# Latent sublayers of a two-layer diffusion trunk: from a raw, then normalised result to an operand normalised in steps behind the first tile pairs

## The chip, the cores and the metric

The kernel runs on one core of a Trainium2 chip. The metric is the device time of one execution in microseconds (us), lower is better. Three runs of the kernel before gave 1200.62, 1200.91 and 1203.27 us; their median is 1200.91 us. One further execution was recorded by the hardware profiler; all rows quoted below come from it.

## What is computed

The reference is a transformer-like trunk with two layers over 256 latent tokens and 256 context tokens of width 1024, all in float32. Each sublayer normalises the stream, scales and shifts it by columns that depend on a conditioning vector, and adds a gated result back:

```
def ffn_sublayer(h, m, g, w13, w2, base):
    hn = modulate(rms_norm(h, g), m[:, :, base], m[:, :, base + 1])
    return h + 0.5 * m[:, :, base + 2] * swiglu(hn, w13, w2)

for i in range(2):
    x = ffn_sublayer(x, ..., 0)          # i = 0: the context too
    x = x + gate * mixer_i(modulate(rms_norm(x)))
    x = ffn_sublayer(x, ..., 6)
return rms_norm(x, final_g)
```

The mixer of layer 0 is windowed attention beside pooling, that of layer 1 a gated three-tap convolution, `W_out(B * conv3(C * x_in))`. The hidden width of a SwiGLU is 2816, or 22 tiles of 128. After layer 0's mixer only the latent tokens are needed, so the last four sublayers (SwiGLU 2 of layer 0, SwiGLU 1 of layer 1, the convolution, SwiGLU 2 of layer 1) work on 256 columns. These four are "latent sublayers"; the change touches only them.

## The kernel before, in words

**Layout.** Everything is transposed: channels lie on the 128 partitions, tokens are the columns of a matmul's moving operand. The stream `x` is `xl_all`, eight blocks (index d or k) of 128 channels by 256 tokens.

**Two-part arithmetic.** The kernel gets float32 accuracy from a faster matmul type (float32r) by splitting each number in two parts, high and low, and adding three products: high·high, high·low and low·high. Weights are split on the chip: `Stream.get` (L80 to L95) hands out weight chunks of 128 x 1024 numbers (eight blocks k of 128 x 128). For each chunk ScalarE casts the raw chunk to `whi` (L100) and VectorE subtracts to get `wlo` (L101). There are four pairs of `whi`/`wlo` buffers, and three raw double chunks in flight from memory on SyncE's queue. So the cast of a chunk can begin when the chunk four places before it has left TensorE, and what it has then is three chunks' time.

**A product of parts, two ways.** `mm3` (L248 to L252) issues three matmuls per block k: `whi` with the operand's high part, `whi` with its low part, `wlo` with the high part. `mm2` (L254 to L261) has the operand's two parts side by side in one tile: one matmul of 512 columns (`whi` with both) and one of 256 (`wlo` with the high part); the two halves of the 512-column result have to be added by whoever reads it. In the last block the 512-column matmul comes last (L261). Before the change `mm2` serves the second half of each SwiGLU (`pz`, L258/L259) and the mixers' output projections (`pwo`).

**Normalising afterwards.** Normalising needs the sum over all channels, known only when the previous sublayer has ended. The first projection of a sublayer does not wait for it: `Act.feed` puts x·gain, not normalised, into the operand tiles `ah` (high) and `al` (low), as soon as a block of the stream is ready, and two further columns 256 and 257 hold the shift. The projections therefore run over 258 columns. The result is normalised when it leaves PSUM: `scaled` (L544 to L550) multiplies by `rs2`, a row of 1/rms per token (1.0 in the two shift columns), and the next instruction adds the shift's product, column 256.

**A SwiGLU (`ffn`).** For f = 0 to 21 ("tile pairs") two chunks, a gate and a value chunk, give `pf`, a PSUM pair (three pairs in turn). `finish` does: `tf` = normalised pair (VectorE, L548), `sl` = Silu (ScalarE, L870), product (VectorE, L871), high part `g` (ScalarE, L872), low part (VectorE, L873). In f = 1 the sums are rooted and spread into `rs2`. Then the second half: for each of eight output blocks d, 22 `mm2` over the pairs `g`, `residual` into `xl_all` (L540) and `feed` of the next sublayer.

**The convolution (`odd_mixer`).** For j = 0 to 7 three chunks: two into `pc` and one into `pb`, then `finish` with `tc`, `zpad`, `y`, `tb`, and an output projection `pwo` of eight blocks of eight `mm2`.

**The modulation columns.** A VectorE dot product (L201, "jk") computes scale, shift and gate columns from weights that stream in by SyncE's queue; a "set" is a load of 1 MB and two such products. 64 sets are spread by credits: `mod_credit(c)` adds c, and a set for the latent tokens costs 2. In `ffn` each pair f from 1 to 21 adds RATE_FFN[0], each chunk of the second half RATE_FFN[1]; in the convolution each j adds RATE_CONV.

**Order.** Inside the latent sublayers the Tile framework's scheduler sets each engine's order from program order, dependencies and priorities (`tc.high_priority`). Each engine takes its instructions in that order.

Of the kernel before, what the change touches and what calls it, by code (L numbers as in the profile page):

```python
# [9 lines left out]
F32 = mybir.dt.float32  # L10
# [7 lines left out]
P = 128  # L18
# [17 lines left out]
NEG = -1e30  # L36
URGENT = 400
RATE_FIRST = (3.3, 1.5)
RATE_FFN = (0.66, 0.7)
RATE_CONV = 0.6  # L40
CH = 8

OPERAND = 4160

C_MODB = 0
C_G = 144
# [71 lines left out]
def hybrid_trunk_kernel(ctx: ExitStack, tc: tile.TileContext, xc, cols_d, modw, wst, poolw_d,  # L118
# [181 lines left out]
    class Act:  # L300
# [39 lines left out]
        def x(self, k, q):  # L340
            return self.hi[:, k, q, :], self.lo[:, k, q, :]

    class Final:
        def __init__(self):
            self.acc = tp.tile([P, 2, T], F32, tag="acc", name="accf", bufs=1)
# [199 lines left out]
    def scaled(pt, rs, n, pool, name):  # L545
        t = pool.tile([P, 544], F32, tag="t", name=f"t{name}", bufs=2)[:, 0:516].rearrange("p (a b) -> p a b", a=2)
        if n:
            nc.vector.tensor_tensor(t[:, 0:n, :], pt[:, 0:n, 0:258], rs, ALU.mult)  # L548
        else:
            nc.vector.tensor_tensor(t[:, 0, :], pt[:, 0:258], rs, ALU.mult)  # L550
        return t

    def lat2(rs):
        return rs[:, 0:1, :].to_broadcast([P, 2, 258])


    def even_mixer(act):
        with tc.tile_pool(name="mix", bufs=2) as ap_:
# [213 lines left out]
            for i in range(4):  # L772
                v = v_turn(i)
                if i + 1 < 4:
                    bias[i + 1] = load_bias(i + 1)
                pr, top, power, weights = scores(i, bias[i])
                if i + 1 < 4:
                    wq = W.get()
                    top(0)
                    top(1)  # L780
                    power(0)
                    power(1)
                    held["q", i + 1] = single(f"pq{i + 1}")
# [12 lines left out]
                    proj_v(i + 1, wv)  # L796
                    po = weigh(i, tn, v)
                    v_finish(i + 1)
                    weigh_finish(i, po)
                    bias_mask(bias[i + 1])  # L800
                    if i == 1:
                        pool_map()
                else:
                    a2 = Act(0, 2, (xl_t,))
# [59 lines left out]
    def ffn(act, l, s, gp, nxt_of, rate1, rate2):  # L864
        g2 = [gp.tile([P, 2, T], F32R, tag=f"g{f}", name=f"g{l}{s}_{f}") for f in range(NF)]

        def finish(f, pt):
            t = scaled(pt, lat2(rs2), 2, gp, f"f{l}{s}{f}")
            sl = gp.tile([P, T], F32, tag="sl", bufs=2, name=f"sl{l}{s}{f}")
            nc.scalar.activation(sl, t[:, 0, 0:256], AF.Silu, bias=t[:, 0, 256:257])  # L870
            nc.vector.scalar_tensor_tensor(sl, t[:, 1, 0:256], t[:, 1, 256:257], sl, ALU.add, ALU.mult)  # L871
            nc.scalar.copy(g2[f][:, 0, :], sl)  # L872
            nc.vector.tensor_tensor(g2[f][:, 1, :], sl, g2[f][:, 0, :].bitcast(F32), ALU.subtract)  # L873

        for f in range(NF):
            pt = pair(f"pf{l}{s}{f}")
            if f == 0:
                ws = W.get(), W.get()
                for ks in (range(KD - 1), range(KD - 1, KD)):
                    for h in range(2):  # L880
                        proj(pt, h, ws[h], act, (0,), ks)
                rr = act.rstd(AF.Silu)
# [24 lines left out]


    def odd_mixer(act, gp, rate):
        y2 = gp.tile([P, KD, 2, T], F32R, name="y2")  # L910
        zs = []
        for b in range(2):
            z = gp.tile([P, T + 32], F32, name=f"zpad{b}")[:, 0 : T + 2]
            nc.gpsimd.memset(z, 0.0)
            zs.append(z)

        def finish(j, pt, pb):
            cw = [cols[:, C_CW + 8 * n + j : C_CW + 8 * n + j + 1] for n in range(3)]
            z = zs[j % 2]
            xi = gp.tile([P, T], F32, tag="sl", bufs=2, name=f"xi{j}")  # L920
            y = gp.tile([P, T], F32, tag="y", bufs=2, name=f"y{j}")
            t = scaled(pt, lat2(rs2), 2, gp, f"c{j}")
            nc.scalar.activation(xi, t[:, 0, 0:256], AF.Identity, bias=t[:, 0, 256:257])
            nc.vector.scalar_tensor_tensor(
                z[:, 1 : T + 1], t[:, 1, 0:256], t[:, 1, 256:257], xi, ALU.add, ALU.mult
            )
# [3 lines left out]
            t = scaled(pb, rs2[:, 0, :], 0, gp, f"b{j}")  # L930
            nc.vector.scalar_tensor_tensor(y, t[:, 0, 0:256], t[:, 0, 256:257], y, ALU.add, ALU.mult)
            nc.scalar.copy(y2[:, j, 0, :], y)
            nc.vector.tensor_tensor(y2[:, j, 1, :], y, y2[:, j, 0, :].bitcast(F32), ALU.subtract)

        for j in range(KD):
            pt, pb = pair(f"pc{j}"), single(f"pb{j}")
            if j == 0:
                ws = W.get(), W.get()
                for ks in (range(KD - 1), range(KD - 1, KD)):
                    for h in range(2):  # L940
                        proj(pt, h, ws[h], act, (0,), ks)
                rr = act.rstd(AF.Silu)
            else:
                for h in range(2):
                    proj(pt, h, W.get(), act, (0,), range(KD))
            w = W.get()
            if j == 0:
                rr.root()
            for k in range(KD):
                mm3(pb[:, 0:258], (w[0][:, k, :], w[1][:, k, :]), act.x(k, 0), k == 0, k == KD - 1)  # L950
            if j == 0:
                rr.spread()
            finish(j, pt, pb)
            mod_credit(rate)
        root_next()
        need_mods(1, 1, 8, 12)
        a2 = Act(1, 2, (xl_t,))
# [6 lines left out]
    act = ffn_first()  # L964
    act = even_mixer(act)
    with tc.tile_pool(name="g1", bufs=1) as gp:
        act = ffn(act, 0, 2, gp, lambda: Act(1, 0, (xl_t,)), *RATE_FFN)
        act = ffn(act, 1, 0, gp, lambda: Act(1, 1, (xl_t,)), *RATE_FFN)
# [134 lines left out]
```

## Time and profile before

| what | value |
|---|---|
| median of three runs | 1200.91 us |
| the profiled execution, its own time | 1201.63 us |
| its span, first to last instruction | 1199.8 us |
| granted TensorE clock, mean over the span | 0.996 |
| weights and other data read | 248.41 MB, 208 GB/s over the span |
| SwiGLU 2 of layer 0, f = 0 to 21 | 517.9 to 652.5 us |
| SwiGLU 1 of layer 1, f = 0 to 21 | 714.5 to 843.0 us |
| convolution, j = 0 to 7 | 905.1 to 975.4 us |
| SwiGLU 2 of layer 1, f = 0 to 21 | 993.2 to 1127.7 us |

How to read the rows: PE is TensorE's matmuls, PEld its weight loads, DVE is VectorE, ACT is ScalarE, SP is SyncE. A row of a timeline gives start, duration, engine, line and operation, and in brackets the idle time before it with what ended it. A matmul's printed duration contains a modelled end and overlaps the next matmul; what a matmul takes of TensorE's time is the distance between starts. A row of grouped instructions ends with count, busy time, mean duration in ns, and the idle time of the engine ahead of them. A row of stages gives for each stretch its length, then each engine's busy time and count, granted clock, share of the DMA engines and GB/s.

### The profile page before, as it was taken

Reading aid. Unit: us, or ns where it says so; the run is one execution under the profiler, and the core shown is the slowest. Engines: PE = TensorE matmul, PEld = TensorE weight load, DVE = VectorE, ACT = ScalarE, POOL = GpSimd, SP = SyncE. Lnnn points to the kernel's source line nnn. Section 1 sums busy time; section 2 is a strip of 40 time slices with the busy share of each in tenths; the row PEclk is TensorE's granted clock in tenths of the full one; section 3 lists DMA queues with packets and bytes.
Section 4 is the critical chain, followed back from the end, with each engine's and each line's share of the span. In section 5 each row is a group of like instructions: output and inputs, shape, how many; then the busy total and the mean of one; then the engine's idle time right before and its main releaser. Section 6 shows DMA issues by size and latency. Waiting matters only on the chain.

```text
span 1199.8 us, 18425 instructions
## 1 busy us (share of the span) xinstructions
PE 1166.3 (97%) x7426; PEld 1041.6 (87%) x7426; DVE 920.2 (77%) x1478; ACT 527.1 (44%) x786; POOL 21.2 (2%) x23
## 2 busy tenths in 40 slices
PE   4999999999999989999999999999999999999997
PEld 2568888888888978789999889999889999999986
DVE  8977686677799577688788988788898888666663
ACT  4352322232344345464445445454545455444542
POOL 2000000000000030000000000000000000000000
PEclk9999999999999999999999999999999999999998
DMA  7764554466676753346776985766884555555541
GB/s 268 256 216 175 176 184 167 156 244 246 265 280 239 204 122 61 106 141 217 260 253 223 335 308 213 262 242 227 306 332 161 207 176 176 178 180 190 189 178 36
DMA packets 45798, 250.65 MB, mean 209 GB/s; under 512 B 12945, under 2 KB 13329, under 8 KB 17553
## 3 DMA queue, kind: packets, MB, share of 16 engines
q1 hardware_dynamic: 45712, 249.48, 59.3%
q8 instruction: 58, 0.95, 0.3%
q14 instruction: 28, 0.22, 0.1%
HBM read 248.41 MB, written 1.05 MB: 208 GB/s over the span
## 4 chain that ended last, share of the span: by engine, by line
PE 93%; DVE 3%; issue 1%; ACT 1%; DMA 0%; SPq 0%; DVEq 0%; ACTq 0%
PE pf L252 11%; PE pf L250 11%; PE pf L251 11%; PE pz L258 10%; PE pa L251 5%; PE pa L252 5%; PE pa L250 5%; PE pz L259 5%; PE p L499 4%; PE py L251 3%; PE py L252 3%; PE py L250 3%; PE pwo L258 1%; PE pc L252 1%; PE pc L250 1%; PE pc L251 1%
## 5 line engine op out<-in xcount | busy, mean ns | idle before, releaser
L100 ACT CAST whi<-raw 128x1024 fp32r<-128x1024 f32 x312 | 327.3, 1050 | 470.9 <-PE pf L251 116.4
L101 DVE TENSOR_TENSOR wlo<-raw,whi 128x1024 fp32r<-128x1024 f32 x312 | 380.1, 1223 | 157.9 <-ACT whi L100 156.7
L252 PE MATMUL pf<-ah,wlo 128*128 128x258 f32 x1056 | 300.9, 285 | 0.0
L250 PE MATMUL pf<-ah,whi 128*128 128x258 f32 x1056 | 300.4, 285 | 0.0
L251 PE MATMUL pf<-al,whi 128*128 128x258 f32 x1056 | 298.2, 282 | 0.0
L201 DVE CUSTOM_DVE_ANT_0 jk<-mr,cvec,cols 128x1024 bf16<-128x1024 f32 x184 | 236.2, 1284 | 2.0 <-DMA mr<-in_modw 0.3
L251 PEld LDWEIGHTS pf<-al,whi 128*128 128x128 f32 x1056 | 202.3, 192 | 0.2
L250 PEld LDWEIGHTS pf<-ah,whi 128*128 128x128 f32 x1056 | 200.7, 190 | 0.0
L252 PEld LDWEIGHTS pf<-ah,wlo 128*128 128x128 f32 x1056 | 200.2, 190 | 0.0
L258 PE MATMUL pz<-g,whi 128*128 128x512 f32 x504 | 178.7, 398 | 0.0
L259 PE MATMUL pz<-g,wlo 128*128 128x256 f32 x528 | 144.3, 281 | 0.0
L258 PEld LDWEIGHTS pz<-g,whi 128*128 128x128 f32 x504 | 94.7, 188 | 22.1
L250 PE MATMUL pa<-xh,whi 128*128 128x512 f32 x288 | 112.0, 389 | 0.0
L252 PE MATMUL pa<-xh,wlo 128*128 128x512 f32 x288 | 112.0, 389 | 0.0
L251 PE MATMUL pa<-xl,whi 128*128 128x512 f32 x288 | 112.0, 389 | 0.0
L259 PEld LDWEIGHTS pz<-g,wlo 128*128 128x128 f32 x528 | 99.7, 189 | 2.2
L250 PE MATMUL py<-gh,whi 128*128 128x512 f32 x176 | 68.5, 389 | 0.0
L251 PE MATMUL py<-gl,whi 128*128 128x512 f32 x176 | 68.5, 389 | 0.0
L252 PE MATMUL py<-gh,wlo 128*128 128x512 f32 x176 | 68.5, 389 | 0.0
L251 PEld LDWEIGHTS pa<-xl,whi 128*128 128x128 f32 x288 | 54.1, 188 | 11.3
L250 PEld LDWEIGHTS pa<-xh,whi 128*128 128x128 f32 x288 | 54.1, 188 | 11.3
L252 PEld LDWEIGHTS pa<-xh,wlo 128*128 128x128 f32 x288 | 54.1, 188 | 11.1
(215 smaller groups left out, 1587.2 us busy)
## 6 DMA issues: line engine op xcount, KB each, us to landing
raw<-in_wst SPq DMA_DIRECT2D x156, 1024.0 KB, 5.1
mr<-in_modw SPq DMA_DIRECT2D x64, 1024.0 KB, 5.1
mr<-in_modw SPq DMA_DIRECT2D x16, 512.0 KB, 5.0
raw<-in_wst SPq DMA_DIRECT2D x8, 512.0 KB, 6.5
bias<-in_rpb SPq DMA_DIRECT2D x32, 64.0 KB, 6.0
xl_all<-in_xc SPq DMA_DIRECT2D x2, 512.0 KB, 7.0
xc_all<-in_xc SPq DMA_DIRECT2D x2, 512.0 KB, 8.4
out<-done SPq DMA_DIRECT2D x3, 256.0 KB, 2.8
```

The source lines that it names most:

```text
L100: nc.scalar.copy(hi, src)
L101: self.last = nc.vector.tensor_tensor(lo, src, hi.bitcast(F32), ALU.subtract).ins
L201: nc.vector.tensor_tensor_reduce(out=junk, in0=raw[:, h, :], in1=cvec[:, q, :], scale=1.0, scalar=cols[:, b : b + 1], op0=ALU.mult, op1=AL ...
L250: nc.tensor.matmul(out, wh, xh, start=first, stop=False)
L251: nc.tensor.matmul(out, wh, xl, start=False, stop=False)
L252: nc.tensor.matmul(out, wl, xh, start=False, stop=last)
L258: nc.tensor.matmul(out, wh, both, start=first, stop=False)
L259: nc.tensor.matmul(out[:, 0:256], wl, x[:, 0, :], start=False, stop=False)
L499: nc.tensor.matmul(pts[j], wf[:, j * P : j * P + P], f32, start=first, stop=last)
```

## The change

`Act` is kept for the parts that also carry context tokens; the latent sublayers use a new class `Lat`.

- `Lat.feed` writes the same x·gain parts, but both into one tile `ah` ("raw").
- `Lat.normalise(d, pool)` makes two blocks (d and d+1) of a normalised operand: multiply the stream by `rs2` (VectorE, 512 elements), scale and shift (two ScalarE activations of 256), high part (ScalarE, 512), low part (VectorE, 512). The parts go side by side into a tile `al`. It is called with d = 0, 2, 4, 6 behind pairs f = 1 to 4 of each SwiGLU and behind j = 0 to 3 of the convolution.
- From pair 6 on (F_RAW), and from j = 4 on (J_RAW), the projection is `wide`: eight `mm2` on that tile. The result needs no normalising and no shift; `joined` adds the two halves: a ScalarE copy out of PSUM and a VectorE addition.
- No credit is given in f = 1 to 5 and j = 0 to 3; the rates become 0.9 per pair (from 0.66) and 1.1 per j (from 0.6).

```
+        def normalise(self, d, pool):
...
+            nc.vector.tensor_tensor(
+                xn, xl_all[:, d : d + 2, :], rs2[:, 0:1, 0:256].to_broadcast([P, 2, T]), ALU.mult
+            )
+            for j in range(2):
+                nc.scalar.activation(
+                    xn[:, j, :], xn[:, j, :], AF.Identity,
+                    bias=mcol[l, s, 0][:, d + j : d + j + 1], scale=gcol[l, s, 0][:, d + j : d + j + 1],
+                )
+            h = self.op[:, d : d + 2, 0, :]
+            nc.scalar.copy(h, xn)
+            nc.vector.tensor_tensor(self.op[:, d : d + 2, 1, :], xn, h.bitcast(F32), ALU.subtract)
+
+    def wide(pt, w, act):
+        for k in range(KD):
+            mm2(pt, (w[0][:, k, :], w[1][:, k, :]), act.op[:, k], k == 0, k == KD - 1)
...
+    def joined(pt, n, pool, name):
+        t = pool.tile([P, 544], F32, tag="t", name=f"t{name}", bufs=2)[:, 0 : n * T].rearrange("p (a b) -> p a b", a=n)
+        nc.scalar.copy(t, pt[:, :, 256:512])
+        nc.vector.tensor_tensor(t, pt[:, :, 0:256], t, ALU.add)
+        return t
...
-RATE_FFN = (0.66, 0.7)
-RATE_CONV = 0.6
+RATE_FFN = (0.9, 0.7)
+RATE_CONV = 1.1
...
             for h in range(2):
                 w = W.get()
                 if f == 1 and h == 0:
                     rr.root()
-                proj(pt, h, w, act, (0,), range(KD))
+                if f < F_RAW:
+                    proj(pt, h, w, act, (0,), range(KD))
+                else:
+                    wide(pt[:, h, :], w, act)
             if f == 1:
                 rr.spread()
                 finish(0, held)
             finish(f, pt)
-            mod_credit(rate1)
+            if 1 <= f <= 4:
+                act.normalise(2 * f - 2, gp)
+            if f >= F_RAW:
+                mod_credit(rate1)
```

**Where instructions stand, TensorE.** The end of the first chunk of pair f = 6 in SwiGLU 2 of layer 0, and the start of its second chunk, in the kernel before (`pf` is the PSUM pair, `ah`/`al` the operand's parts, `whi`/`wlo` the weight's):

```order
L250 MATMUL pf_4618<-ah_3886,whi_4517 128x258
L251 MATMUL pf_4618<-al_3887,whi_4517 128x258
L252 MATMUL pf_4618<-ah_3886,wlo_4518 128x258
L250 MATMUL pf_4618<-ah_3886,whi_4555 128x258
L251 MATMUL pf_4618<-al_3887,whi_4555 128x258
L252 MATMUL pf_4618<-ah_3886,wlo_4556 128x258
```

The same place in the changed kernel, where `al` now holds both parts of the normalised operand:

```order
L260 MATMUL pf_4635<-al_4346,whi_4528 128x512
L261 MATMUL pf_4635<-al_4346,wlo_4529 128x256 x2
L263 MATMUL pf_4635<-al_4346,whi_4528 128x512
L260 MATMUL pf_4635<-al_4346,whi_4572 128x512
L261 MATMUL pf_4635<-al_4346,wlo_4573 128x256
```

Three matmuls of 258 columns per block have become one of 512 and one of 256; nothing else moved in between.

**VectorE at the convolution's fourth group.** The last part of j = 3 in the kernel before (`tc`, `tb` come out of PSUM, `zpad` and `y` are the convolution, `wlo` the weight split):

```order
L548 TENSOR_TENSOR tc_8838<-pc_8748,rs_97 128x516
L101 TENSOR_TENSOR wlo_8809<-raw_8646,whi_8808 128x1024
L924 SCALAR_TENSOR_TENSOR zpad_8419<-tc_8838,xi_8836 128x256
L927 TENSOR_SCALAR y_8837<-zpad_8419,cols 128x256
L550 TENSOR_TENSOR tb_8845<-pb_8749,rs_97 128x258
L929 SCALAR_TENSOR_TENSOR y_8837<-zpad_8419,cols,y_8837 128x256 x2
L101 TENSOR_TENSOR wlo_8855<-raw_8646,whi_8854 128x1024
L931 SCALAR_TENSOR_TENSOR y_8837<-tb_8845,y_8837 128x256
```

The same in the changed kernel, where L390 and L400 are the first and the last instruction of the step that normalises blocks 6 and 7:

```order
L1012 TENSOR_SCALAR y_8415<-zpad_7986,cols 128x256
L613 TENSOR_TENSOR tb_8423<-pb_8327,rs_97 128x258
L1014 SCALAR_TENSOR_TENSOR y_8415<-zpad_7986,cols,y_8415 128x256
L390 TENSOR_TENSOR xn_8428<-xl_all,rs_97 128x512
L1014 SCALAR_TENSOR_TENSOR y_8415<-zpad_7986,cols,y_8415 128x256
L103 TENSOR_TENSOR wlo_8439<-raw_8218,whi_8438 128x1024
L1017 SCALAR_TENSOR_TENSOR y_8415<-tb_8423,y_8415 128x256
L400 TENSOR_TENSOR al_8101<-xn_8428,al_8101 128x2x256
```

The normalising step stands behind `tb`, which reads the group's last PSUM result, and ahead of the group j = 4 that needs it.

**TensorE at the convolution's fifth group.** In the kernel before the two chunks of `pc` in j = 4 follow each other:

```order
L250 MATMUL pc_8850<-ah_7828,whi_8750 128x258
L251 MATMUL pc_8850<-al_7829,whi_8750 128x258
L252 MATMUL pc_8850<-ah_7828,wlo_8751 128x258
L250 MATMUL pc_8850<-ah_7828,whi_8780 128x258
L251 MATMUL pc_8850<-al_7829,whi_8780 128x258
```

In the changed kernel six blocks of the first `pc` chunk are followed by six of the `pb` chunk, and only then by blocks 6 and 7 of `pc`:

```order
L260 MATMUL pb_8435<-al_8101,whi_8386 128x512
L261 MATMUL pb_8435<-al_8101,wlo_8387 128x256
L260 MATMUL pc_8434<-al_8101,whi_8328 128x512
L261 MATMUL pc_8434<-al_8101,wlo_8329 128x256 x2
L263 MATMUL pc_8434<-al_8101,whi_8328 128x512
L260 MATMUL pc_8434<-al_8101,whi_8358 128x512
```

So twelve blocks' matmuls, not six, stand between the group's start and the first use of operand blocks 6 and 7.

More of the change, by code (lines that the diff above doesn't have):

```diff
@@ L341, in x, with __init__, feed, rstd @@
             return self.hi[:, k, q, :], self.lo[:, k, q, :]
+    class Lat:
+        def __init__(self, l, s):
+            need_mods(l, s, 0, 8)
+            self.l, self.s, self.name = l, s, f"{l}{s}"
+            self.raw = xp.tile([P, OPERAND], F32R, tag="ah", name=f"ah{l}{s}")[:, 0 : KD * 516].rearrange(
+                "p (k a t) -> p k a t", k=KD, a=2)
+            self.acc = tp.tile([P, 2, T], F32, tag="acc", name=f"acc{l}{s}", bufs=1)
+            sh = mcol[l, s, 0][:, 0:8].unsqueeze(2).to_broadcast([P, KD, 2])
+            h = self.raw[:, :, 0, 256:258]
+            nc.scalar.copy(h, sh)
+            nc.vector.tensor_tensor(self.raw[:, :, 1, 256:258], sh, h.bitcast(F32), ALU.subtract)
+        def feed(self, d):
+            with tc.high_priority(offset=URGENT):
+                x = xl_t[d]
+                g = gcol[self.l, self.s, 0][:, d : d + 1]
+                h = self.raw[:, d, 0, 0:256]
+                acc = self.acc[:, 0, :]
+                sq = acc if d == 0 else tp.tile([P, T], F32, tag="sq0", name=f"sq{self.name}0{d}", bufs=2)
+                nc.scalar.activation(h, x, AF.Copy, scale=g)
+                nc.vector.scalar_tensor_tensor(
+                    self.raw[:, d, 1, 0:256], x, g, h.bitcast(F32), ALU.mult, ALU.subtract
+                )
+                nc.scalar.activation(sq, x, AF.Square)
+                if d:
+                    nc.vector.tensor_tensor(acc, acc, sq, ALU.add)
+        def rstd(self):
+            return Rstd([self.acc[:, 0, :]], 256, self.name, AF.Silu)
+        def x(self, k, q):
+            return self.raw[:, k, 0, :], self.raw[:, k, 1, :]
+        def normalise(self, d, pool):
+            l, s = self.l, self.s
+            if d == 0:
+                self.op = xp.tile([P, OPERAND], F32R, tag="al", name=f"al{l}{s}")[:, 0 : KD * 512].rearrange(
+                    "p (k a t) -> p k a t", k=KD, a=2)
+            xn = pool.tile([P, 544], F32, tag="t", name=f"xn{l}{s}{d}", bufs=2)[:, 0:512].rearrange(
+                "p (a b) -> p a b", a=2)
+            nc.vector.tensor_tensor(
[5 more added lines that the diff above has]
+                    bias=mcol[l, s, 0][:, d + j : d + j + 1], scale=gcol[l, s, 0][:, d + j : d + j + 1],
+                )
+            h = self.op[:, d : d + 2, 0, :]
+            nc.scalar.copy(h, xn)
+            nc.vector.tensor_tensor(self.op[:, d : d + 2, 1, :], xn, h.bitcast(F32), ALU.subtract)
@@ L888, in ffn @@
                     rr.root()
-                proj(pt, h, w, act, (0,), range(KD))
+                if f < F_RAW:
+                    proj(pt, h, w, act, (0,), range(KD))
+                else:
+                    wide(pt[:, h, :], w, act)
             if f == 1:
@@ L941, in odd_mixer @@
                         proj(pt, h, ws[h], act, (0,), ks)
-                rr = act.rstd(AF.Silu)
+                rr = act.rstd()
+            elif j < J_RAW:
+                for h in range(2):
+                    proj(pt, h, W.get(), act, (0,), range(KD))
             else:
                 for h in range(2):
-                    proj(pt, h, W.get(), act, (0,), range(KD))
+                    wide(pt[:, h, :], W.get(), act)
             w = W.get()
@@ L948, in odd_mixer @@
                 rr.root()
-            for k in range(KD):
-                mm3(pb[:, 0:258], (w[0][:, k, :], w[1][:, k, :]), act.x(k, 0), k == 0, k == KD - 1)
+            if j < J_RAW:
+                for k in range(KD):
+                    mm3(pb[:, 0:258], (w[0][:, k, :], w[1][:, k, :]), act.x(k, 0), k == 0, k == KD - 1)
+            else:
+                wide(pb, w, act)
             if j == 0:
@@ L953, in odd_mixer @@
             finish(j, pt, pb)
-            mod_credit(rate)
+            if j < 4:
+                act.normalise(2 * j, gp)
+            if j >= J_RAW:
+                mod_credit(rate)
         root_next()
         need_mods(1, 1, 8, 12)
-        a2 = Act(1, 2, (xl_t,))
+        a2 = Lat(1, 2)
         proj_out = OutProj(y2, 1, a2, ODD_OUT)
```

43 lines of the change are left out of this document (28 added, 15 removed).

## The prediction

> **What bounds the kernel now.** I read the page first (busy shares and the chain that ended last), then the stages, then TensorE's starts inside stages.
>
> ```profile
> PE 1166.3 (97%) x7426; PEld 1041.6 (87%) x7426; DVE 920.2 (77%) x1478; ACT 527.1 (44%) x786; POOL 21.2 (2%) x23
> PE 93%; DVE 3%; issue 1%; ACT 1%; DMA 0%; SPq 0%; DVEq 0%; ACTq 0%
> ```
>
> TensorE is busy nearly all the time and carries 93% of the chain. Since matmuls overlap, "busy" does not yet say that none waits; for that I look at the latent sublayers stage by stage: pairs f = 2 to 5 of SwiGLU 2 of layer 0, its later pairs, its second half, then the convolution's j = 1 to 3 and j = 4 to 7.
>
> ```profile
> core 0: us, PE busy (x) PEld busy (x) DVE busy (x) ACT busy (x) POOL busy (x), PEclk, DMA share, GB/s
> 536.40:559.60 23.20, 23.20 (x194) 23.20 (x194) 18.59 (x27) 11.87 (x18) 0.00 (x0) 1.00 0.65 228
> 565.50:652.40 86.90, 86.90 (x720) 86.90 (x719) 70.01 (x105) 42.68 (x60) 0.00 (x0) 1.00 0.68 242
> 652.50:714.50 62.00, 62.00 (x354) 53.89 (x353) 57.16 (x93) 31.09 (x41) 0.00 (x0) 1.00 0.88 319
> 914.36:940.52 26.16, 26.16 (x219) 26.16 (x217) 24.32 (x42) 12.24 (x17) 0.00 (x0) 1.00 0.56 189
> 940.52:975.40 34.88, 34.88 (x291) 34.88 (x289) 27.90 (x45) 15.46 (x20) 0.00 (x0) 1.00 0.52 181
> ```
>
> In each, TensorE's busy time equals the stretch and the granted clock is 1.00. VectorE is next, with 80% to 93%. Does anything else set the pace? The waits of the weight stream say no:
>
> ```profile
> ACT whi L100 <- PE pf L251: 116.4, 76, 1.8
> ACT whi L100 <- PE pz L258: 63.0, 42, 1.8
> ```
>
> ScalarE's cast of a weight chunk waits for TensorE to release a buffer, not the other way round. So in these stages time is the number of matmuls times their distance, and that is where the change acts.
>
> **The distance of the two matmul patterns.** Now the starts. First a stretch of the old pattern, three matmuls of 258 columns per block: a group of the convolution, j = 1.
>
> ```profile
> 914.36 0.29 PE L250 MATMUL pc<-ah,whi 128*128 128x258 f32 x1
> ...
> 923.08 0.29 PE L250 MATMUL pc<-ah,whi 128*128 128x258 f32 x1
> ```
>
> Between these starts lie three chunks of eight blocks, 72 matmuls: 8.72 us, so 2.907 us per chunk. The pattern of one 512 and one 256 exists in two places. The last two whole output blocks of the convolution's projection (8 blocks k each):
>
> ```profile
> 987.40 0.40 PE L261 MATMUL pwo<-y,whi 128*128 128x512 f32 x1
> ...
> 993.01 0.40 PE L261 MATMUL pwo<-y,whi 128*128 128x512 f32 x1
> ```
>
> 5.61 us for 16 blocks, or 2.805 us per eight. And the whole second half of SwiGLU 1 of layer 1, 8 x 22 = 176 blocks:
>
> ```profile
> 843.00 0.40 PE L258 MATMUL pz<-g,whi 128*128 128x512 f32 x1
> ...
> 905.06 0.28 PE L250 MATMUL pc<-ah,whi 128*128 128x258 f32 x1
> ```
>
> 62.06 us, or 2.821 us per eight. Weights, chunk layout and the position of the last 512-column matmul in `pwo` are those of the new projections, so I lean to it and take 2.81 us.
>
> **The change, part by part.**
>
> *New projections.* Pairs 6 to 21 are 16 pairs of 2 chunks in three SwiGLUs, 96 chunks; j = 4 to 7 are 4 groups of 3, 12 chunks. 108 chunks x (2.907 - 2.81) = 10.5 us less; by `pz` 9.3, by `pwo` 11.0. All of it lies on the path that sets the end as long as TensorE stays the engine waited for. Where does the gain come from? Not mainly from columns: 774 become 768 per block, 0.8%, while the rows give 3%. One matmul start fewer per block carries the rest. The Trainium skill ("TensorE: Matmul & The Clock Gate", section "Back-to-back issue gap") gives the distance of warm matmuls as N/2.4 + 2.5 ns; an estimate from it is that a block goes from 330 to 325 ns and the 864 blocks gain 4.3 us instead of 10.5. The trace disagrees with it in size: it has 363 ns (2.907 us / 8) and 351 ns.
>
> *The normalising steps.* Durations of the nearest forms, and of what stands in each pair already:
>
> ```profile
> L101 DVE TENSOR_TENSOR wlo<-raw,whi 128x1024 fp32r<-128x1024 f32 x312 | 380.1, 1223 | 157.9 <-ACT whi L100 156.7
> L100 ACT CAST whi<-raw 128x1024 fp32r<-128x1024 f32 x312 | 327.3, 1050 | 470.9 <-PE pf L251 116.4 <-PE pa L251 114.1 <-PE pz L258 63.0
> L201 DVE CUSTOM_DVE_ANT_0 jk<-mr,cvec,cols 128x1024 bf16<-128x1024 f32 x184 | 236.2, 1284 | 2.0 <-DMA mr<-in_modw 0.3
> L548 DVE TENSOR_TENSOR tf<-pf,rs 128x516 f32<-128x516 f32 x66 | 45.8, 694 | 21.5 <-PE pf L252 20.5 <-ACT rs L296 0.9
> L871 DVE SCALAR_TENSOR_TENSOR sl<-tf,sl 128x256 f32<-128x256 f32 x66 | 31.6, 479 | 0.0
> L873 DVE TENSOR_TENSOR g<-sl,g 128x256 fp32r<-128x256 f32 x66 | 27.9, 423 | 21.3 <-ACT g L872 21.3
> L439 DVE TENSOR_TENSOR s<-s,pa 128x512 f32<-128x512 f32 x18 | 12.3, 682 | 0.0
> L441 DVE TENSOR_TENSOR gl<-s,gh 128x512 fp32r<-128x512 f32 x22 | 15.1, 686 | 3.5 <-ACT gh L440 3.4
> L440 ACT CAST gh<-s 128x512 fp32r<-128x512 f32 x22 | 13.7, 622 | 24.9 <-DVE s L439 24.9
> L438 ACT ACTIVATE s<-pa 128x512 f32<-128x512 f32 x18 | 10.6, 589 | 0.0
> L328 ACT ACTIVATE ah<-xl_all,g 128x256 fp32r<-128x256 f32 x40 | 20.3, 509 | 27.9 <-DVE xl_all L529 14.7 <-DVE xl_all L540 13.1
> ```
>
> One step is two VectorE operations of 512 (2 x 0.686 = 1.37 us) and on ScalarE 2 x 0.509 + 0.622 = 1.64 us. Sixteen steps put 22 us on VectorE and 26 us on ScalarE, beside TensorE's matmuls. What hides them is VectorE's spare time, and it has to be enough in that stage: in f = 2 to 5, 18.59 us of 23.20 are used, with one modulation set (2 x 1.284 = 2.6 us) that is moved away; 18.59 - 2.6 + 4 x 1.37 = 21.5 us (all four steps run in this stretch), 93%. In the convolution's j = 1 to 3 it is tight: 24.32 - 2.6 + 3 x 1.37 (the fourth step runs in j = 4) = 25.8 of 26.16 us, 99%. Overlapping starts make the real load a little less, queue waits make it more. VectorE takes its instructions in order, so behind each step's last subtraction (it waits for two activations and a cast on ScalarE) stand the next `wlo` and the parts of `g` or `y`. The reserve against that is the four weight buffers: a cast released at the end of a chunk is needed three chunks, 8.7 us, later.
>
> *The entry into the new operand.* In a SwiGLU the last step stands behind pair 4 and pair 6 begins a whole pair (5.8 us) later: no wait. In the convolution it stands behind `tb`, which waits for the end of j = 3: then about 0.4 us `tb`, 0.5 `y`, 0.7 the multiplication, 1.0 two activations, 0.6 cast, 0.7 subtraction, 3.9 us, and on VectorE meanwhile two more `y` operations and a `wlo`. TensorE first does twelve blocks, 12 x 0.351 = 4.2 us. If VectorE is late, which 99% makes likely, one wait follows. I bound it by 0 and 2.5 us (two late `wlo`) and take 1.0.
>
> *The result of pairs 6 and later.* VectorE: `tf` with 0.694 becomes an addition of 512 out of PSUM (0.68), `sl` a plain product, nearer the 0.423 of L873 than 0.479: about 0.1 us less per pair. ScalarE gets a copy of 512 out of PSUM, 0.59 us, and has room for it: 42.68 of 86.90 us. But it stands in ScalarE's queue ahead of a weight cast, and waits for the pair's end. The way from there is 0.59 + 1.05 (cast) + 0.68 + 1.22 (`wlo`) = 3.5 us, with a modulation set between 6.1, and the chunk is needed after 8.4 us. No wait; the last pair's way to `g` is longer by that 0.59 and is needed only 21 blocks, 7.4 us, after the pair.
>
> *Modulation sets.* Their number stays 64. From pair 6 on 0.9 of credit is 0.45 set per pair. VectorE's own part there: 70.01 us less five sets at 2.6 over 15 pairs is 3.8 us per pair; with 0.45 x 2.6 it is 5.0 of the new 5.62 us, 89%. The second half already runs at 57.16 of 62.00 us, 92%, with TensorE never waiting, so this is bearable. SyncE's queue gets the loads of 1 MB later and closer; the 242 GB/s of the stage rise towards 270, below the 319 of the second half.
>
> *The raw parts in one tile, the two shift columns:* same bytes, same instructions, no cost. The rest of the kernel is unchanged.
>
> **Sum.** -10.5 + 1.0 = -9.5 us. Against the profiled execution (1201.63 us, of which the span is 1199.8) that is 1192.1 us; this execution lay 0.72 us above the median, so I predict 1191.4 us for the median.
>
> **The rivals.** *Lost at the entries (0.10).* VectorE falls behind in the steps and TensorE waits at all four entries, or the weights come late behind them. At 1.0 to 1.5 us each, 4 to 6 us are lost: 1200.9 - 10.5 + 4 to 6 = 1194.4 to 1196.4 us. For it: 99% in the convolution, the new ScalarE round trip in each pair. Against: the pair of reserve in the SwiGLUs and the second half, which runs without a wait at the same load.
>
> *Only columns count (0.05).* If the new projections ran at the old price per column, because their operand tile behaves unlike `pwo`'s, the gain is 108 x 2.907 x 6/774 = 2.4 us, and with the wait of 1.0 us the time is 1199.5 us: no difference. Against it stand both measured stretches. The rule of the Trainium skill cited above ("TensorE: Matmul & The Clock Gate") points this way, with its 4.3 us.
>
> *The weight stream runs dry (0.04), slower.* Place: pairs with a modulation set. VectorE's load there is 3.8 + 2.6 = 6.4 us, and its addition now waits for ScalarE's copy, 0.59: 7.0 us against 5.62, 1.4 more than the pair gives; normally the next pair makes up for it. If the reserve were gone, each of the 15 sets (14 in two SwiGLUs, one in the convolution) would stop TensorE by 1.4 us, 21 us in all: 1200.9 - 10.5 + 21 = 1211.4 us, slower. It decides from the point where the way of 6.1 us exceeds 8.4, that is with 2.3 us of further queueing. Against it: the second half carries 92% without a wait.
>
> **How the numbers follow.** Forecast 0.81, with a range of its own from 1189.2 (by `pwo`, no wait, and 0.7 us for the runs' spread) to 1193.5 (by `pz`, a wait of 2). The range to hold the time 8 in 10 goes from 1189.0 to 1195.5: it leaves out the last two rivals, most of the first, and small tails. A measurement of this kernel can tell about 0.2%, 2.4 us, from no change. Below 1198.5 lie the forecast, the first rival and part of the doubt: faster 0.91, same 0.05, slower 0.04.
>
> **What would show it.** Right: starts of consecutive first matmuls of pairs 6 to 21 lie 5.6 us apart (5.81 before), VectorE near 93% in f = 2 to 5 and 89% in later pairs, casts still waiting for TensorE. A gap of TensorE at j = 4 between 0 and 2.5 us and none at pair 6. Wrong: TensorE's gaps ahead of `al` in pair 6, or ahead of `wlo` in pairs with a set; or 2.88 us per new chunk without any gap. The prediction falls if the time is above 1198.5 us.

## The result and the profile after

The changed kernel takes 1190.74 us (median of four runs, 1190.12 to 1193.23) against 1201.21 us for four runs of the kernel before: ratio 0.9914, 95% interval 0.9895 to 0.9932. It is faster by 10.5 us, or 0.9%; the prediction was 1191.4. (Of all executions reported below one, of the kernel with the padded operand, took 2188 us at a granted clock of 0.86; it is left out of every comparison.) The profiled execution took 1190.12 us with a span of 1188.3, 11.5 us less than before's span. I account for the change against these two spans, where the starts of single instructions can be compared.

The profile page of the changed kernel, busy times and chain:

```profile
PE 1155.3 (97%) x6562; PEld 990.7 (83%) x6562; DVE 930.9 (78%) x1510; ACT 572.8 (48%) x886; POOL 21.2 (2%) x23
PE 93%; DVE 3%; issue 1%; ACT 1%; DMA 0%; SPq 0%; DVEq 0%; ACTq 0%
```

864 matmuls fewer, and TensorE still carries 93% of the chain. The stages that the prediction read, in the same order (pairs 2 to 5, later pairs, second half, j = 1 to 3, j = 4 to 7):

```profile
535.58:558.46 22.88, 22.88 (x194) 22.88 (x193) 20.68 (x30) 18.39 (x30) 0.00 (x0) 1.00 0.59 203
564.10:648.60 84.50, 84.50 (x481) 73.51 (x480) 70.63 (x110) 48.77 (x76) 0.00 (x0) 1.00 0.73 258
648.75:710.70 61.95, 61.95 (x353) 53.88 (x352) 58.30 (x95) 31.16 (x41) 0.00 (x0) 1.00 0.87 325
907.25:932.99 25.74, 25.74 (x218) 25.74 (x217) 25.03 (x42) 17.43 (x26) 0.00 (x0) 1.00 0.56 181
932.99:966.93 33.94, 33.94 (x194) 29.41 (x193) 29.36 (x52) 18.41 (x27) 0.00 (x0) 1.00 0.55 191
```

TensorE fills every stage as before; VectorE is at 90, 84, 94, 97 and 87%. So the time is still matmuls times distance. The new pattern, six chunks of the convolution (j = 5 and 6):

```profile
941.55 0.40 PE L260 MATMUL pc<-al,whi 128*128 128x512 f32 x1
...
958.47 0.40 PE L260 MATMUL pc<-al,whi 128*128 128x512 f32 x1
```

16.92 us / 6 = 2.820 us per chunk: the value of `pz`, not the 2.805 read from `pwo`. (The 5.61 us of `pwo` were a block of 2.79 and one of 2.82: in the trace of before the matmul between them starts at 990.19 us.) And the old pattern where the changed kernel still uses it (j = 1, three chunks):

```profile
907.25 0.28 PE L252 MATMUL pc<-ah,whi 128*128 128x258 f32 x1
...
915.83 0.28 PE L252 MATMUL pc<-ah,whi 128*128 128x258 f32 x1
```

8.58 us / 3 = 2.860 us, where the same matmuls took 2.907 before. Nothing in the prediction said that.

The sum: 108 new chunks x (2.907 - 2.820) = 9.4 us; 48 old chunks x (2.907 - 2.860) = 2.3 us; the wait at j = 4 cost 0.1 us, and one wait in the convolution's output projection is 1.5 us where it was 1.2. That makes 11.3 us. Stage by stage the traces give a little less to the change: 0.5 of the 11.5 us lie ahead of everything that was changed (SwiGLU 2 of layer 0 begins at 517.42 us instead of 517.94), so about 11 us are its own, 0.3 less than the sum.

### The profile page after: what moved, and what is told of

Read it like the earlier page. It is cut to its first block, busy times and chain, and to the rows that moved or that the text cites. A ratio compares the mean times of both kernels' runs of the same rounds, so it can differ in the third digit from the quotient of the medians.

```text
span 1188.3 us, 16777 instructions
## 1 busy us (share of the span) xinstructions
PE 1155.3 (97%) x6562; PEld 990.7 (83%) x6562; DVE 930.9 (78%) x1510; ACT 572.8 (48%) x886; POOL 21.2 (2%) x23
## 4 chain that ended last, share of the span: by engine, by line
PE 93%; DVE 3%; issue 1%; ACT 1%; DMA 0%; SPq 0%; DVEq 0%; ACTq 0%
PE pf L260 13%; PE pz L260 10%; PE pf L261 8%; PE pa L254 6%; PE pa L253 5%; PE pa L252 5%; PE pz L261 5%; PE p L562 4%; PE py L254 3%; PE py L253 3%; PE py L252 3%; PE pf L253 3%; PE pf L252 3%; PE pf L254 3%; PE pf L263 2%; PE pwo L260 2%
## 5 line engine op out<-in xcount | busy, mean ns | idle before, releaser
L260 PE MATMUL pf<-al,whi 128*128 128x512 f32 x672 | 241.0, 397 | 0.0
L261 PE MATMUL pf<-al,wlo 128*128 128x256 f32 x768 | 199.9, 281 | 0.0
L261 PEld LDWEIGHTS pf<-al,wlo 128*128 128x128 f32 x768 | 145.0, 189 | 8.9
L260 PEld LDWEIGHTS pf<-al,whi 128*128 128x128 f32 x672 | 126.4, 188 | 26.2
L253 PE MATMUL pf<-ah,whi 128*128 128x258 f32 x288 | 81.6, 283 | 0.0
L252 PE MATMUL pf<-ah,whi 128*128 128x258 f32 x288 | 80.9, 281 | 0.0
L254 PE MATMUL pf<-ah,wlo 128*128 128x258 f32 x288 | 80.8, 281 | 0.0
L619 ACT COPY tf<-pf 128x512 f32<-128x512 f32 x48 | 28.1, 586 | 73.4 <-PE pf L263 73.4
L253 PEld LDWEIGHTS pa<-xl,whi 128*128 128x128 f32 x288 | 54.1, 188 | 11.3
```

Source lines behind the costliest of these rows:

```text
L252: nc.tensor.matmul(out, wh, xh, start=first, stop=False)
L253: nc.tensor.matmul(out, wh, xl, start=False, stop=False)
L254: nc.tensor.matmul(out, wl, xh, start=False, stop=last)
L260: nc.tensor.matmul(out, wh, both, start=first, stop=False)
L261: nc.tensor.matmul(out[:, 0:256], wl, x[:, 0, :], start=False, stop=False)
L619: nc.scalar.copy(t, pt[:, :, 256:512])
```

## The experiments

Theory at this point: two gains, not one. The new product saves its 87 ns per chunk, and putting the raw parts into one tile makes the old product cheaper, for a reason that has to do with where the operand lies. Rivals: the layout is worth nothing by itself and the early pairs got cheaper because the modulation sets moved away; or the gain hangs on both together.

**One tile alone.** In the kernel before, for the latent sublayers:

```
+                both = xp.tile([P, OPERAND], F32R, tag="ah", ...)[:, 0 : KD * 516].rearrange(
+                    "p (k a t) -> p k a t", k=KD, a=2)
+                self.hi, self.lo = both[:, :, 0:1, :], both[:, :, 1:2, :]
```

> The kernel before with one thing of the change: in the latent sublayers the raw operand's high and low parts lie in one tile, the low part 258 columns behind the high part. Still three matmuls of 258 columns in every projection, no normalising steps, modulation sets where they were. Theory A (the new product alone pays, where the parts lie is worth nothing): 1201 us, 2.907 us per chunk. Theory B (where the parts lie in the partition changes the distance of the old matmuls): 2.860 us per chunk as in the changed kernel's early pairs, 156 chunks x 0.047 = 7.3 us less, 1193.9 us. Theory C (the early pairs got cheaper because the modulation sets moved away): 1201 us.

Measured: 1194.51 us, ratio 0.9944 (0.9928 to 0.9961), span 1192.6. Starts of j = 1 and j = 2:

```profile
910.05 0.28 PE L250 MATMUL pc<-ah,whi 128*128 128x258 f32 x1
...
918.63 0.28 PE L250 MATMUL pc<-ah,whi 128*128 128x258 f32 x1
```

8.58 us for three chunks, 2.860 each. Theory B holds, A and C fall: an address change alone, with the same instructions in the same number (7426 matmuls in both), is worth 7.2 us of span (156 x 0.047 = 7.3).

**The steps without the new product.**

```
-F_RAW = 6
-J_RAW = 4
+F_RAW = 99
+J_RAW = 99
...
-            if f >= F_RAW:
+            if f >= 6:
                 mod_credit(rate1)
```

(likewise `j >= 4`). The normalised operand is computed and not read.

> The changed kernel without the new product: raw parts in one tile, the normalising steps run and the sets stand where the change puts them, but every projection uses three matmuls of 258 columns, and nothing reads the normalised operand. Theory A: 1201 us and whatever the steps cost. Theory B: 2.860 us per chunk everywhere, 1193.9 us, as the one-tile run if the steps are hidden; above it by what the steps cost if they are not. Theory C: 2.860 in pairs 0 to 5 and j = 0 to 3 and 2.907 later, 48 x 0.047 = 2.3 us less, 1198.9 us.

Measured: 1194.98 us, ratio 0.9949 (0.9934 to 0.9964), span 1192.9. That is 0.3 us of span more than one tile alone: the sixteen normalising steps are hidden, as predicted. Against this kernel the new product gains 1192.9 - 1188.3 = 4.6 us (108 x (2.860 - 2.820) = 4.3).

**The new product with the old layout.** The reverse of the first experiment: `Lat` keeps `ah` and `al` as in the kernel before, the normalised operand lies in a tile `op`, and the convolution's output, to make room, in tiles of the SwiGLUs:

```
-            self.raw = xp.tile([P, OPERAND], F32R, tag="ah", ...)
+            self.hi, self.lo = (xp.tile([P, OPERAND], F32R, tag=t, ...)... for t in ("ah", "al"))
...
-                self.op = xp.tile([P, OPERAND], F32R, tag="al", ...)
+                self.op = pool.tile([P, KD * 512], F32R, tag="op", ...)
```

> The changed kernel with its layout undone and the new product kept: the raw operand's parts lie in two tiles as in the kernel before, the normalised operand in a tile of its own (the convolution's output takes its room from the SwiGLU's tiles). If layout and new product are two separate gains: the early pairs and j = 0 to 3, 48 chunks, go back to 2.907 us, 48 x 0.047 = 2.3 us more than the changed kernel, 1193.0 us, and the new chunks stay at 2.820. If the new product depends on the raw parts' layout too, its chunks change as well and the time is off this by several us.

Measured: 1191.92 us, ratio 0.9923 (0.9909 to 0.9938), span 1190.0. The two patterns, first j = 1, then j = 5:

```profile
907.97 0.29 PE L252 MATMUL pc<-ah,whi 128*128 128x258 f32 x1
...
916.69 0.29 PE L252 MATMUL pc<-ah,whi 128*128 128x258 f32 x1
...
942.71 0.40 PE L260 MATMUL pc<-op,whi 128*128 128x512 f32 x1
...
951.17 0.40 PE L260 MATMUL pc<-op,whi 128*128 128x512 f32 x1
```

8.72 / 3 = 2.907 and 8.46 / 3 = 2.820. Each pattern keeps its own value. In spans: before 1199.8, layout alone 1192.6, product alone 1190.0, both 1188.3. Alone the layout gains 7.2 us and the product 9.8; together they gain 11.5, because 108 of the 156 chunks that the layout helps are then of the new kind.

**Is it the common tile or the shifted start?** The low part stays in its own tile `al`, but starts 258 columns into each block. In the kernel before:

```
+            if len(xs) == 1:
+                self.lo = self.lo[:, :, 1:2, :]
```

> The kernel before with the low part still in its own tile, but starting 258 columns into each block's 516, so that its address differs from the high part's by 1032 bytes plus a constant, where before the two addresses differed by a constant alone. Theory B1 (what pays in the one-tile layout is the low part's shifted start): 2.86 us per chunk, about 1194.5 us as the one-tile run. Theory B2 (it pays that both parts lie in one tile, near each other): 2.907 us per chunk, 1201 us.

Measured: 1195.14 us, ratio 0.995 (0.9933 to 0.9966). Starts of j = 2 and j = 3:

```profile
919.32 0.28 PE L250 MATMUL pc<-ah,whi 128*128 128x258 f32 x1
...
927.92 0.28 PE L250 MATMUL pc<-ah,whi 128*128 128x258 f32 x1
```

8.60 / 3 = 2.867. The shifted start gives 0.040 of the 0.047 us (B1); one tile is not needed. The next two runs show that the shift is one way to the gain and not the only one.

**Which addresses?** Two placements in the kernel before, two tiles each:

```
+                    xp.tile(...)[:, 0 : 0 + KD * 284].rearrange("p (k q t) -> p k q t", k=KD, q=1)[:, :, :, 0:258]
```

> The kernel before with the parts of block k at a distance of 284 columns instead of 516, in two tiles as before. Before, the three matmuls of a block take about 349 ns for k = 3 and 7 and 362 to 373 for the others. Theory B (the operand's address within a line of 64 bytes counts): a block starts 48k bytes past a multiple of 64 instead of 16k, so the cheap blocks are now k = 1 and 5; the time stays at about 1201 us. Rival D (the weights' address counts, 512 bytes per block): the cheap blocks stay 3 and 7.

```
+                    xp.tile(...)[:, 12 : 12 + KD * 272].rearrange("p (k q t) -> p k q t", k=KD, q=1)[:, :, :, 0:258]
```

> The kernel before with the parts of every block starting 48 bytes past a multiple of 64 (distance 272 columns, first block 12 columns in), in two tiles. Theory B: every block takes about 350 ns, 2.80 us per chunk, 156 x 0.107 = 16.7 us less, about 1184.5 us. Rival D and theory A: as before, 1201 us.

Measured, one execution each: 1196.59 and 1196.80 us (spans 1194.8 and 1195.0). In j = 2 a chunk takes 2.880 and 2.870 us (8.64 and 8.61 us for three), with both parts of a block at the same column of their tiles. What a block's three matmuls take in the first chunk of j = 1, in ns from start to start, k = 0 to 7:

```
before        369 367 374 349 366 363 367 351
one tile      359 358 359 356 359 355 360 357
284 apart     363 357 359 358 357 368 360 366
272 apart     361 359 359 367 359 352 351 367
```

Both placements are faster than before's, but neither expectation holds: with 284 columns the cheap blocks are not 1 and 5, nor do they stay at 3 and 7, and with every block 48 bytes past a multiple of 64 the blocks still differ by 16 ns, and not all are cheap. The start within 64 bytes is not what decides. Nor does the place alone: with 272 columns the times of single blocks do not stay with k. The next two chunks of j = 1 have 356 361 366 348 362 359 358 368 and 358 353 351 367 356 361 366 348, a pattern that repeats every twelve blocks, where the operand's places repeat every eight. And in the first of the three SwiGLUs the same kernel, its operand in the same two tiles, settled into another pattern, every four blocks, and another price. Twelve chunks there, and twelve in the next SwiGLU:

```profile
547.35 0.28 PE L250 MATMUL pf<-ah,whi 128*128 128x258 f32 x1
...
582.07 0.28 PE L250 MATMUL pf<-ah,whi 128*128 128x258 f32 x1
...
737.16 0.28 PE L250 MATMUL pf<-ah,whi 128*128 128x258 f32 x1
...
771.62 0.28 PE L250 MATMUL pf<-ah,whi 128*128 128x258 f32 x1
```

34.72 us against 34.46, or 2.893 and 2.87 per chunk. So a placement seems to act through the pattern into which the stream settles, and what sets that pattern stays open.

**The normalised operand 520 columns apart.** Its blocks in the changed kernel were 512 columns apart:

```
-                ...[:, 0 : KD * 512].rearrange("p (k a t) -> p k a t", k=KD, a=2)
+                ...[:, 0 : KD * 520].rearrange("p (k r) -> p k r", k=KD)[:, :, 0:512].rearrange("p k (a t) -> p k a t", a=2)
```

> The changed kernel with the blocks of the normalised operand 520 instead of 512 columns apart. If the distance of these matmuls depends on the operand's place as that of the 258-column ones did (1.6% between two placements), a chunk leaves 2.820 us by up to 0.05 either way and the time moves by up to 108 x 0.05 = 5 us. If matmuls of 512 and 256 columns do not mind: 2.820 and 1190.7 us. I expect the first with 0.5, its sign open.

Measured: 1189.55 us, the median of three, ratio 0.9903 (0.9883 to 0.9922), span 1187.1. Starts of j = 6 and j = 7:

```profile
949.16 0.39 PE L260 MATMUL pc<-al,whi 128*128 128x512 f32 x1
...
957.58 0.40 PE L260 MATMUL pc<-al,whi 128*128 128x512 f32 x1
```

8.42 / 3 = 2.807: the place counts here too, 13 ns per chunk, or 1.4 us for 108 chunks. Span and median gain 1.2 us each, which these intervals do not separate from the changed kernel.

**And the raw parts 260 columns apart as well.** On top of the padded operand, the raw tile (its blocks thereby lie 520 columns apart instead of 516):

```
-            self.raw = xp.tile(...)[:, 0 : KD * 516].rearrange("p (k a t) -> p k a t", k=KD, a=2)
+            self.raw = xp.tile(...)[:, 0 : KD * 520].rearrange("p (k a t) -> p k a t", k=KD, a=2)[:, :, :, 0:258]
```

> The changed kernel with the normalised operand's blocks 520 columns apart (as in the padded run, 2.807 us per chunk) and the raw parts 260 columns apart instead of 258. If only the normalised operand's place matters here, 1189.6 us as the padded run. If the raw parts' distance matters too, their 48 chunks leave 2.860 us by up to 0.05 either way, up to 2.4 us. Below both kernels in either case if the padded run's gain is real.

Measured: 1190.90 us, ratio 0.9916 (0.9901 to 0.993), span 1188.4. The new chunks stay at 2.807, the old ones go to 2.873 at j = 2 and 3 (2.882 at j = 1). By the chunks that costs 48 x 0.013 = 0.6 us; the span grows by 1.3 us over the padded run, and the rest lies outside these chunks. It beats the kernel before, not the changed one; the padded run alone is the fastest measured, by a margin inside the noise.

**Modulation sets left where they were.**

```
-RATE_FFN = (0.9, 0.7)
-RATE_CONV = 1.1
+RATE_FFN = (0.66, 0.7)
+RATE_CONV = 0.6
...
-            if f >= F_RAW:
-                mod_credit(rate1)
+            mod_credit(rate1)
```

(likewise in the convolution)

> The changed kernel with the modulation sets where they were: credit in every pair and every j at the old rates 0.66 and 0.6. VectorE then has 18.6 + 4 x 1.37 = 24.1 us of work in the 23.2 us of pairs 2 to 5 and 28.4 in the 26.2 us of j = 1 to 3. Reserve theory (a cast has three chunks' time, 8.4 us or more, so a stage may run over by some us): 1190.7 us, at most 1 us more. Rival (VectorE's load there decides): 0.9 us lost in each of three SwiGLUs and 2.2 us or more in the convolution, 1195.6 us, with TensorE waiting for wlo or al at pair 6 and j = 4.

Measured: 1191.40 us, ratio 0.9918 (0.9904 to 0.9933). Pairs 2 to 5 and j = 1 to 3 in this kernel:

```profile
535.00:557.90 22.90, 22.90 (x193) 22.85 (x192) 21.46 (x33) 18.02 (x31) 0.00 (x0) 1.00 0.64 219
906.31:932.06 25.75, 25.75 (x219) 25.75 (x218) 25.41 (x44) 16.58 (x24) 0.00 (x0) 1.00 0.58 191
```

VectorE is at 94 and 99% there, with one set in each stretch, and no pair of a SwiGLU is held up. Only the convolution's entry is, by this row (the brackets tell the idle time and what ended it):

```profile
939.11 0.50 PE L260 MATMUL pc<-al,whi 128*128 128x512 f32 x1 [0.64 <-DVE al L400]
```

The rival falls. The reserve theory is only half tested: the load that was to exceed the stretches (24.1 us in 23.2, 28.4 in 26.2) measured 21.46 us in 22.90 and 25.41 in 25.75. In these traces moving the sets was worth 0.7 us, in one place (j = 4 takes 9.26 us instead of 8.56); in the whole time, 0.7 us by the medians, it does not stand clear of the noise.

**Three weight buffers instead of four.** In the changed kernel, and the same in the kernel before as the measure:

```
-    wp_s = ctx.enter_context(tc.tile_pool(name="wsplit", bufs=4))
+    wp_s = ctx.enter_context(tc.tile_pool(name="wsplit", bufs=3))
...
-    W = Stream(nc, wp_raw, wp_s, wst, 6, 3)
+    W = Stream(nc, wp_raw, wp_s, wst, 6, 2)
```

> The changed kernel with three instead of four weight buffers and the split two instead of three chunks ahead: the time from a cast's release to its use falls from 8.4 to 5.6 us in the new projections. If the reserve is what hides the copy out of PSUM and the sets (way of 3.5 us, with a set 6.1), only pairs with a set stop TensorE, by about 0.5 us each, 14 pairs: 7 us over the changed kernel, beside what the kernel before loses by the same. If the way is much shorter than I count: as the changed kernel beside that.

> The kernel before with three weight buffers and the split two chunks ahead, as the measure for the changed kernel with three. Its way from release to use is 2.3 us (cast, subtraction), with a set 4.9, against 5.8 us: no loss in the latent sublayers beyond 1 us; elsewhere (attention mixer, output projections) up to 5 us, the same in both.

Measured: 1192.44 us (0.9926, 0.991 to 0.9943) for the changed kernel, 1202.50 us (1.0012, 1.0 to 1.0023) for the kernel before. By the ratios (0.9914 to 0.9926, and 1 to 1.0012) three buffers cost either kernel 0.0012, or 1.4 us, which does not stand clear of the noise; they are not 7 us apart. In the changed kernel's trace TensorE waits twice in the convolution, at its entry and once in j = 5 (0.42 us), and nowhere in the SwiGLUs' pairs; the row of the entry:

```profile
933.73 0.38 PE L261 MATMUL pb<-al,wlo 128*128 128x256 f32 x1 [0.75 <-DVE wlo L103]
```

So in the SwiGLUs the weight stream was not near running dry: no pair waited with the 5.6 us that three buffers leave, so the way from release to use is shorter than the 6.1 us that I added up.

**New product one pair earlier.** Credit from pair 6 on, as in the changed kernel:

```
-F_RAW = 6
+F_RAW = 5
...
-            if f >= F_RAW:
+            if f >= 6:
```

> The changed kernel with the new product from pair 5 on, so that it begins right behind pair 4, whose end the last normalising step follows: no pair of reserve. The scheduler then puts six blocks of pair 5, six of pair 6 and only then blocks 6 and 7. Forecast's step (the way from the pair's end to the last part is about 3.9 us and twelve blocks give 4.1): 0 to 1 us lost in each SwiGLU against 6 chunks x 0.040 = 0.24 us gained, 1190.5 to 1193.5 us. Entry rival (VectorE is late by 1.5 us more at each entry): 4.5 us lost, 1195 us.

Measured: 1191.51 us, ratio 0.992 (0.9904 to 0.9937), span 1188.8. The entry, where the last part is written and read:

```profile
556.43 0.69 DVE L400 TENSOR_TENSOR al<-xn,al 128x512 fp32r<-128x512 f32 x1 [0.34 <-ACT al L399]
...
556.89 0.79 PE L260 MATMUL pf<-al,whi 128*128 128x512 f32 x2
557.51 0.28 PE L261 MATMUL pf<-al,wlo 128*128 128x256 f32 x1
```

The second of the two matmuls of 512 starts when `al` is written. The two take 0.62 us; a matmul of 512 takes 0.23 elsewhere in this stretch, so about 0.15 us is lost. The pair of reserve was not needed: the scheduler fills the way with the next pair's blocks. The entry rival, 4.5 us, falls.

## Why the prediction was right, point by point

**What bounds it.** Right. TensorE fills every stage in both kernels, and each kernel's time follows the number and distance of its matmuls.

**New projections: -10.5 us.** Right in kind, too large in size: -9.4 us. The step that failed is "so I lean to it and take 2.81 us": the new chunks take 2.820, as the row of `pz` had it, although weights and layout are those of `pwo`. The padded operand took 2.807, so a difference of this size between two places of the operand is nothing unusual.

**Where that gain comes from.** "One matmul start fewer per block carries the rest" is half wrong. In the changed kernel the old block takes 2.860 / 8 = 357.5 ns and the new one 352.5: 5.0 ns. That is the difference, 330 to 325, which follows from the gap of single warm matmuls, N/2.4 + 2.5 ns, that the Trainium skill gives ("TensorE: Matmul & The Clock Gate", section "Back-to-back issue gap"). The runs agree with it for these two places, though not in the level, which is 27 ns higher; with the padded operand (2.807 / 8 = 350.9) the difference is 6.6 ns, so the close agreement is in part luck. The other 5.9 ns per block of the 10.9 went with the old operand's place and not with the new product. I had set the Trainium skill's difference against a measured one without asking whether the two measured stretches differed in anything but the pattern.

**"The raw parts in one tile ... same bytes, same instructions, no cost."** This step failed. It changes what every remaining old matmul takes: 2.3 us in the changed kernel by the chunks (1.7 by the spans 1190.0 and 1188.3), 7.2 us when it is the only change. I had counted instructions and bytes, and not looked at whether the distance of equal matmuls depends on their operand. The trace of before could have warned me: in its first chunk of j = 1 blocks of identical shape differ between 349 and 374 ns, in a pattern of k.

**Normalising steps hidden.** Right: 0.3 us of span (steps alone against one tile alone). 93% was forecast for VectorE in pairs 2 to 5 and 90% measured, 99 and 97% in j = 1 to 3, 89 and 84% in the later pairs. These start 5.64 us apart, where 5.6 was forecast, and TensorE shows no gap at pair 6. The forms cost what the neighbours cost: in the changed kernel

```profile
L390 DVE TENSOR_TENSOR xn<-xl_all,rs 128x512 f32<-128x512 f32 x16 | 10.9, 683 | 0.0
L400 DVE TENSOR_TENSOR al<-xn,al 128x512 fp32r<-128x512 f32 x16 | 11.1, 691 | 3.1 <-ACT al L399 3.1
L399 ACT CAST al<-xn 128x512 fp32r<-128x512 f32 x16 | 10.0, 622 | 0.4
L394 ACT ACTIVATE xn<-xn,m,g 128x256 f32<-128x256 f32 x32 | 17.5, 595 | 1.9 <-DVE xn L390 1.3
L619 ACT COPY tf<-pf 128x512 f32<-128x512 f32 x48 | 28.1, 586 | 73.4 <-PE pf L263 73.4
L620 DVE TENSOR_TENSOR tf<-pf,tf 128x512 f32<-128x512 f32 x48 | 33.1, 690 | 24.7 <-ACT tf L619 24.7
L946 DVE TENSOR_TENSOR sl<-tf,sl 128x256 f32<-128x256 f32 x48 | 20.1, 419 | 0.0
```

against 0.686, 0.622, 0.509 (the activation with scale and bias is 0.09 dearer), 0.59, 0.68 and 0.42.

**The entry of the convolution: +1.0 us.** Mis-sized, 0.1. The chain, VectorE first, then TensorE's first use of blocks 6 and 7, in the changed kernel:

```profile
933.22 0.42 DVE L613 TENSOR_TENSOR tb<-pb,rs 128x258 f32<-128x258 f32 x1
933.55 0.48 DVE L1014 SCALAR_TENSOR_TENSOR y<-zpad,cols,y 128x256 f32<-128x256 f32 x1
933.94 0.69 DVE L390 TENSOR_TENSOR xn<-xl_all,rs 128x512 f32<-128x512 f32 x1
934.55 0.48 DVE L1014 SCALAR_TENSOR_TENSOR y<-zpad,cols,y 128x256 f32<-128x256 f32 x1
934.94 1.22 DVE L103 TENSOR_TENSOR wlo<-raw,whi 128x1024 fp32r<-128x1024 f32 x1
936.08 0.48 DVE L1017 SCALAR_TENSOR_TENSOR y<-tb,y 128x256 f32<-128x256 f32 x1
936.51 0.69 DVE L400 TENSOR_TENSOR al<-xn,al 128x512 fp32r<-128x512 f32 x1
...
937.26 0.50 PE L260 MATMUL pc<-al,whi 128*128 128x512 f32 x1
```

From the end of j = 3 at 932.99 the last part takes 4.2 us and the twelve blocks 4.2. VectorE at 97% was hardly late: `tb` starts 0.2 us after j = 3 has ended, and the reserve of twelve blocks took up the rest.

**Modulation sets, the copy out of PSUM.** Right that they cost nothing; the two buffer runs and the run with the sets unmoved show that the reserve in the SwiGLUs would have covered more.

**The total** came out near (-9.5 forecast, -10.5 in the medians, -11.5 in the spans), but partly by luck. The terms missed by 1.1 us (the product, taken too high), -2.3 (the layout, put at nothing), -0.9 (the entry) and 0.3 (the output projection's wait), -1.8 in sum: errors of both signs hid each other, and the medians lie 1.0 us nearer to the forecast than the spans.

## What to carry to other kernels

When TensorE is the bound, read the distance between starts for each matmul form in the trace, and check whether equal matmuls are equally far apart; where they are not, try other places for the operand before changing the arithmetic. Here that change of a few lines was worth 7.2 us alone, where sixteen normalising steps and a new product were worth 9.8 alone and add 4.3 on top of it. Before a gain is laid to an instruction pattern, compare the two patterns on operands in the same place. And look at the reserve before fearing a busy engine off the path: VectorE at 97% cost 0.1 us here, with four buffers and twelve blocks ahead of the consumer.

## What the runs showed of the hardware that was not expected

Eight blocks of three matmuls of 258 float32r columns took from 2.860 to 2.907 us when only the place of their moving operand was changed (2.867 with the low part shifted in its own tile, 2.873 with the parts 260 columns apart, 2.880 with the blocks 284 apart in two tiles); eight pairs of one of 512 and one of 256 took 2.807 or 2.820. The start modulo 64 bytes is not the cause: for the two placements tried to explain it, single blocks still ranged from 351 to 368 ns. The place alone does not fix the time either: with the blocks 272 columns apart the same tiles gave 2.893 us in one SwiGLU and 2.871 in the other two.

Settled streams repeat after whole numbers of a step of 6.667 ns, to within 0.01 of it in means over 20 and more repeats of a pattern: a chunk takes 436 steps before (2906.67 ns), 429 in one tile (2860.00), 430 with the low part shifted (2866.67), 432 with 284 columns (2880.00), 423 and 421 for the two new ones (2820.00, 2806.67); with 272 columns four blocks take 217 (1446.67) and twelve 646 (4306.67). What makes these steps, and why a place leads to one number and not another, was not found.
